# Experts two at a time, 32 places each, with each weight block read as one 8 KB row per partition

## The chip, the cores and the metric

The kernel runs on one core of one Trainium2 chip. The metric is device time in microseconds (us). TensorE does the matrix products (the profile calls it PE, and its weight loads PEld), VectorE is DVE, ScalarE is ACT, GpSimd is POOL, and SyncE is SP. SP issues nearly all transfers from HBM; 16 DMA engines carry them out.

## The reference

The program is three transformer blocks over 256 tokens of 1024 features, all in float32. The first two have a mixer of several attention kinds and a dense feed-forward part. The third has two attentions and then a mixture of 32 experts, which is the part that the change touches:

```
g_top = argmax(h @ w_group)                    # one of 4 groups per token
e_w, e_idx = top_k(softmax(h @ w_router of that group), 2)   # 2 of its 8 experts
for e in range(32):
    a = silu(h @ w_e_gate[e]) * (h @ w_e_up[e])   # 1024 -> 512
    out = out + gates[:, e] * (a @ w_e_down[e])   # 512 -> 1024
x = rmsnorm(x + out)
```

Every expert has three matrices of 2 MB, so that the experts' weights are 192 blocks of 1 MB (1024 KB each). A token uses only 2 of 32 experts, 16 tokens per expert on average; in the reference's routing of these inputs (seed 0) the fullest expert gets 24.

## The kernel before

The dense products of all blocks and the experts draw their weights from one stream (class `Stream`). A unit of it is up to 1 MB, kept in a place of 8 KB on each of the 128 partitions. `pump` issues transfers on SP's queue in the order of use, as long as there is a place; `free` gives a unit's place back after its last product, and calls `pump`. In the experts' stage there are 15 places, and three more (`LENT`) that serve for a single unit each. So a transfer can wait on SP for the product that last read its place.

`plan2` lists the experts' units: for each expert gate and up for the first 512 input features, gate and up for the other 512, then two units of the down matrix. The down units of the last two experts come last. A gate or up unit holds four rows of 2 KB on a partition, 128 matrix rows apart; a down unit two rows of 4 KB.

`route` finds for each token and expert the token's place among the expert's tokens. An expert has `CAP` = 64 places. `t_batch` gathers four experts at once: one-hot matrices on VectorE, and 32 products that lay the tokens' features on the partitions (`xe`, 256 columns, 64 for each expert); it also makes the matrices `gt` that bring results back. It runs as a side task, spread over the steps of the main loop. Nothing of the main loop starts before the first two pieces of batch 0.

`moe` (L2249) is the main loop, one expert at a time. For each of two halves of the input features, and each of four pieces of 128, it issues two products with 64 columns of stationary tokens and 512 moving columns of weights: gate into rows 0:64 of a PSUM bank, up into rows 64:128. These are two column tiles of TensorE. After the first half comes `emit_down` of the expert before (L2206), after the second `t_act` (tanh, two products on VectorE, four transposes, a copy on ScalarE), and after each second expert `emit_scatter` (L2233), four full-width products that add the results to the sum in PSUM. Before the last expert a branch on all engines (L2265) goes to `overflow` (L2043) if any expert has more than `CAP` tokens; that path runs every expert over all tokens again. `last_norm` (L2308) ends the program.

A float32 product of 512 columns shows as two records of the profile. Instructions issued through the class `Timed` all bear line 252, so that they are told apart by their tiles.

Of the kernel before, what the change touches and what calls it, by code (L numbers as in the profile page):

```python
# [13 lines left out]
P = 128  # L14
# [10 lines left out]
CAP = 64  # L25
NE = 32

# [21 lines left out]
LENT = 3  # units of the experts' weights that come into the arena while it has room  # L49
# [3 lines left out]
class Tables:  # L53
    """Tables that depend on the shapes alone, side by side: name -> (column, width)."""
# [17 lines left out]
def _tables():  # L72
    f = np.float32
    p, j = np.arange(P), np.arange(P)
    # for the whole program
# [7 lines left out]
    # for the first blocks  # L83
# [51 lines left out]
    # for the attention of the last block: distance to each key, or BIG where there is no such key  # L135
# [15 lines left out]
class Stream:  # L151
    """Weights in the order of their use: raw tiles come ahead by DMA, and the tiles of the dense
    products are split into two float32r parts a few pieces ahead of the product."""
# [24 lines left out]
    def pump(self, n=99):  # L178
        while self.issued < len(self.units) and self.slots and n:
            n -= 1  # L180
            self.held[self.issued] = self.slots.pop(0)
            view = self.slot(self.issued)
            for c, w, src in self.units[self.issued][2]:
                self.nc.sync.dma_start(out=view[:, :, c : c + w], in_=src)
            self.issued += 1
# [41 lines left out]
class Timed:  # L227
    """An engine whose instructions also move a rough clock, by which the order of emission is chosen."""
# [27 lines left out]
    def price(self, method, args, kw):  # L256
# [8 lines left out]
        if self.name == "PE":  # L265
            if method == "transpose":
                return 0.107 * n / 128
            if kw["lhsT"].dtype == F32R:
                return n / 2370 if n >= 256 else n / 600
            return max(0.213, n / 592) * (0.5 if out.shape[0] <= 64 else 1)  # L270
# [26 lines left out]
class Side:  # L297
    """Work that is emitted between the steps of the dense products: a step of a task when the steps
    before it are through by the rough clock, so that no engine's queue waits for another task."""

    def __init__(self):
# [6 lines left out]
        self.task = None  # [earliest start, end]; None: the dense products  # L308
        self.ahead = False  # weights are split ahead of their use
# [56 lines left out]
    def blocks(self, c0, dims, size):  # L366
        """The blocks of 8 bytes of a partition that an access touches."""
# [68 lines left out]
    def step(self, now):  # L436
        """Each task whose time has come goes on by a step."""
# [57 lines left out]
class Arena:  # L495
    """First-fit space in SBUF tiles; what may follow what is tracked by region."""
# [67 lines left out]
class Kernel:  # L564
# [26 lines left out]
    def split(self, hi, lo, ps, scale=1.0):  # L591
        """hi + lo = ps * scale, each a float32r."""
# [9 lines left out]
    def pow(self, out, in_):  # L602
        """in_ ** -0.5"""
# [24 lines left out]
    # groups of columns of the first blocks' w_in: (mode, name, column, width)  # L628
# [42 lines left out]

    def norm_row(self, k, gain):
        """Features k of x transposed, times their gain, in two parts."""
# [20 lines left out]
    def norm_rstd(self, rstd, ssq=None, scale=None):  # L694
        """(mean of the squares, times scale squared, + EPS) ** -0.5"""
# [49 lines left out]
    def banks(self, gi):  # L745
        """Four banks until the first norm is there, if there is room for it, then three of them."""
# [3 lines left out]
    def accs(self, segs, gi):  # L750
        """Accumulators of a group in two of the four banks of the dense products."""
# [53 lines left out]
    def t_wide(self):  # L805
        """rstd of each token along the free dimension, on all partitions."""
# [175 lines left out]
    def gelu2(self, out, x, tmp):  # L982
        """out = 2 gelu(x), tanh form; x may be in PSUM."""
# [12 lines left out]
    def rope(self, eng, z, n, which, dsts):  # L996
        """z [P, 2, n heads, 64] -> dsts (same shape)"""
# [21 lines left out]
    def t_qk(self, l):  # L1019
        """Rotated queries and keys, features on the partitions."""  # L1020
# [56 lines left out]
    def t_O(self, l):  # L1077
        """Room for the results of pairs of heads: two in a bank."""
# [12 lines left out]
    def t_branch(self, l, hp, br):  # L1091
        """Two heads of the selected or the window branch."""
# [68 lines left out]
        # back in their own place, the keys on the partitions  # L1161
# [18 lines left out]
    def t_pair(self, l, hp):  # L1180
        """The three branches' sum."""
# [11 lines left out]
    def t_gla(self, l):  # L1193
# [45 lines left out]
        # ex[:, i, 0]: level i (0: 128, 1..7: 64..1); ex[:, i, 1]: level i + 1, 7: 128  # L1239
# [182 lines left out]
    def t_params(self, l):  # L1422
        """Small parameters of a layer that need a transposition."""
# [36 lines left out]
    def next_norm(self, half, gain, l, tag):  # L1460
        """After half of x is final."""
# [21 lines left out]
    def norm_x(self, half):  # L1483
        """Half of x times the gains of the norm between the blocks, and its squares' sum."""
# [23 lines left out]
    def ffn(self, l, next_gain, next_tag):  # L1508
# [6 lines left out]
        for c in range(DFF // 256):  # L1515
            # gate and up, a bank each, the features on the partitions
# [9 lines left out]
            def go(c=c, g=g, u=u):  # L1526
                """silu(g) u in two parts"""
# [24 lines left out]
    def plan2(self):  # L1552
        """256 columns each: (mode, what, column)"""
# [14 lines left out]
        self.exp_units = [[] for _ in range(NE)]  # L1568

        def rows(e):  # L1570
            for h in range(2):
                for name in ("w_e_gate_2", "w_e_up_2"):
                    src = self.A[name][0][e][h * 512 : h * 512 + 512, :].rearrange("(k p) c -> p k c", p=P)
                    self.exp_units[e].append(self.st.add(512, 4, [(0, 512, src)], split=False))

        def down(e):
            for h in range(2):
                src = self.A["w_e_down_2"][0][e][h * 256 : h * 256 + 256, :].rearrange("(k p) c -> p k c", p=P)
                self.exp_units[e].append(self.st.add(D, 2, [(0, D, src)], split=False))

        for e in range(NE):
            rows(e)
            if e < NE - 2:
                down(e)
        down(NE - 2)
        down(NE - 1)
# [81 lines left out]
    def t_att(self, needs, groups, sink, slot, drops):  # L1668
        """Two heads: a softmax over the keys of all groups. groups: (queries, keys, values, distances,
        slopes of the two heads), each made when it is there."""  # L1670
# [79 lines left out]
        for gi, (need, q, k, v, dist, slopes) in enumerate(groups):  # L1750
# [6 lines left out]
            # back in their own place, the keys on the partitions  # L1757
# [79 lines left out]
    def mix2(self):  # L1837
        """x += (sigmoid(gate_d) (y_d W_d) + sigmoid(gate_s) (y_s W_s)) W_out"""
# [97 lines left out]
    def route(self):  # L1936
        """Of each token and expert: the place among the expert's tokens, from 1 (0: none), and the
        gate, which is made later."""
# [19 lines left out]
        def top(v, n, oh):  # L1958
            """The first of the largest of n: its value and its place as a one-hot."""
# [41 lines left out]
        # the group's share 1 / gs, of it the larger 1 / (1 + v), the other v / (1 + v)  # L2001
# [22 lines left out]
    def t_most(self):  # L2024
        """The largest place, in a register of each engine."""
# [581 lines left out]
```

## Time and profile before

| | |
|---|---|
| Time, median of 3 runs | 1522.21 us (1521.21 to 1523.0) |
| Span of the profiled execution | 1516.3 us, 5.9 below that median |
| TensorE busy | 1430.1 us, 94% of the span |
| VectorE, ScalarE, GpSimd busy | 52%, 39%, 15% |
| DMA | 360.78 MB, mean 238 GB/s |
| Experts' weights, by the size of their units | 192 x 1024 KB, 201.3 MB |

The span runs from the first to the last instruction. The page gives only the span of the profiled execution; the time of a run has launch and end around it, and the difference of 5.9 us is taken for that. Busy is the time in which an engine has any instruction under way. Matrix products overlap each other, so that a busy TensorE may still be able to do more. The DMA share is the time that packets took, summed over 16 engines; since packets overlap on an engine it can pass 1.

### The profile page before, as it was taken

How to read it: one execution, taken by the hardware profiler on the slowest of the kernel's cores; microseconds unless marked ns; L12 is line 12 of the kernel's file. 1: busy time of each engine (PE TensorE's matmuls, PEld its weight loads, DVE VectorE, ACT ScalarE, POOL GpSimd, SP SyncE). 2: the span in 40 equal slices, each digit the busy share in tenths (PEclk: the TensorE clock that was granted, in tenths of full speed). 3: DMA queues.
4: the chain of work that ended last, by engine and by line, in shares of the span. 5: the costliest groups of instructions: out<-in, count | busy, mean ns of one | idle time of the engine just before them, and what ended most of it. 6: DMA issues, size and time to landing. Idle time of an engine off the chain costs nothing. (4 is left out here: it accounts for less than half of the span.)

```text
span 1516.3 us, 23640 instructions
## 1 busy us (share of the span) xinstructions
PE 1430.1 (94%) x9055; PEld 1028.1 (68%) x9055; DVE 787.2 (52%) x1641; ACT 589.0 (39%) x1227; POOL 222.6 (15%) x341
## 2 busy tenths in 40 slices
PE   8789999999989999999999999979999999999996
PEld 7677999988767999988898998733333333333332
DVE  4487677756586777756766655642212121121212
ACT  5526655555535655555645465311111110111111
POOL 1144111101154111113523020110000000000000
PEclk9998999999999999999999999979999999999998
DMA  8652555547451556466344444879999999999993
GB/s 271 214 174 78 158 184 188 177 158 221 130 194 57 181 181 193 171 209 191 109 143 140 140 148 158 319 284 355 335 390 393 396 393 393 395 393 394 395 391 126
DMA packets 215049, 360.78 MB, mean 238 GB/s; under 512 B 8673, under 2 KB 106482, under 8 KB 214802
## 3 DMA queue, kind: packets, MB, share of 16 engines
q1 hardware_dynamic: 213362, 354.92, 66.9%
q0 software_dynamic: 1104, 3.58, 0.8%
q8 instruction: 72, 1.18, 0.3%
q10 hardware_dynamic: 464, 0.71, 0.1%
q14 instruction: 47, 0.39, 0.1%
HBM read 358.14 MB, written 1.05 MB: 237 GB/s over the span
## 5 line engine op out<-in xcount | busy, mean ns | idle before, releaser
L252 DVE TENSOR_TENSOR wlo<-raw,whi 128x512 fp32r<-128x512 f32 (+3 forms) x560 | 406.7, 734 | 263.1 <-ACT whi L252 251.0
L252 ACT CAST whi<-raw 128x512 fp32r<-128x512 f32 (+3 forms) x560 | 336.9, 605 | 351.2 <-PE psum L252 318.2
L252 PE MATMUL psum<-h_hi,whi 128*128 128x256 f32 x1040 | 296.1, 285 | 2.7 <-ACT whi L252 2.7
L252 PE MATMUL psum<-h_lo,whi 128*128 128x256 f32 x1040 | 290.8, 280 | 0.1
L252 PE MATMUL psum<-h_hi,wlo 128*128 128x256 f32 x1040 | 290.8, 280 | 0.0
L252 PE MATMUL psum<-raw,arena 128*64 128x512 f32 x712 | 227.0, 609 | 10.2 <-ACT arena L252 7.0
L252 DVE COPY arena<-psum 128x512 f32<-128x512 f32 (+4 forms) x96 | 57.4, 598 | 333.1 <-ACT arena L252 223.5
L252 PEld LDWEIGHTS psum<-h_hi,whi 128*128 128x128 f32 x1040 | 196.1, 189 | 10.0 <-issue 4.8
L252 PEld LDWEIGHTS psum<-h_lo,whi 128*128 128x128 f32 x1040 | 196.2, 189 | 0.9 <-issue 0.5
L252 PEld LDWEIGHTS psum<-h_hi,wlo 128*128 128x128 f32 x1040 | 196.0, 188 | 0.2 <-DVE wlo L252 0.2
L252 PE MATMUL psum<-raw_right,arena 128*64 128x512 f32 x504 | 166.3, 603 | 5.7 <-ACT arena L252 5.4
L252 ACT COPY arena<-psum 128x512 f32<-128x512 f32 (+3 forms) x89 | 48.2, 542 | 288.0 <-PE psum L252 275.0
L252 PE MATMUL psum<-arena 64*128 64x128 f32 (+11 forms) x732 | 144.8, 400 | 13.4 <-DVE arena L252 10.9
L252 PE MATMUL psum<-whi,h_hi 128*128 128x256 f32 (+3 forms) x448 | 146.0, 326 | 1.4 <-ACT arena_o L252 1.1
L252 PE MATMUL psum<-wlo,h_hi 128*128 128x256 f32 (+3 forms) x448 | 138.1, 308 | 0.0
L252 PE MATMUL psum<-whi,h_lo 128*128 128x256 f32 (+3 forms) x448 | 137.9, 308 | 0.0
L252 PEld LDWEIGHTS psum<-raw,arena 128*64 128x64 f32 x712 | 64.3, 139 | 97.1 <-issue 80.6
L252 PEld LDWEIGHTS psum<-arena 64*128 64x128 f32 (+4 forms) x732 | 75.2, 180 | 68.5 <-issue 42.4
L252 PE MATMUL psum<-raw_left,arena 128*64 128x512 f32 x296 | 111.4, 609 | 3.1 <-ACT arena L252 3.1
L252 ACT ACTIVATE arena<-psum 64x512 f32<-64x512 f32 (+3 forms) x70 | 33.7, 481 | 181.7 <-PE psum L252 175.8
L252 PEld LDWEIGHTS psum<-raw_right,arena 128*64 128x64 f32 x504 | 46.8, 137 | 72.6 <-issue 64.1
L252 PEld LDWEIGHTS psum<-whi,h_hi 128*128 128x128 f32 x448 | 85.1, 190 | 11.2 <-issue 4.3
(233 smaller groups left out, 1897.5 us busy)
## 6 DMA issues: line engine op xcount, KB each, us to landing
raw<-in_w_in_dram SPq DMA_DIRECT2D x76, 512.0 KB, 4.9
raw<-in_w_e_gate_dram SPq DMA_DIRECT2D x31, 1024.0 KB, 11.8
raw<-in_w_e_up_dram SPq DMA_DIRECT2D x31, 1024.0 KB, 10.0
raw<-in_w_e_down_dram SPq DMA_DIRECT2D x27, 1024.0 KB, 13.9
raw_right<-in_w_e_down_dram SPq DMA_DIRECT2D x23, 1024.0 KB, 13.0
raw<-in_w_gate_dram SPq DMA_DIRECT2D x44, 512.0 KB, 4.0
raw<-in_w_up_dram SPq DMA_DIRECT2D x44, 512.0 KB, 5.0
raw<-in_w_down_dram SPq DMA_DIRECT2D x20, 1024.0 KB, 5.1
```

Source lines behind the costliest of these rows:

```text
L252: return f(*args, **kw)
```

## The change

`CAP` becomes 32. Experts go in pairs (`q` of 16, `NQ = NE // 2`): four products at a time, gate and up of two experts, each with 32 stationary columns into its own 32 rows of the PSUM bank. A batch of the gather has eight experts of 32 places, a scatter serves four experts. The units come in the order gate, up of one expert, gate, up of the other, for each half; then four down units. Each unit is read as one run of 8 KB per partition (four neighbouring matrix rows instead of four that lie 128 apart), and the operands that meet it are taken with a step of 4, or 2, to match. The branch to `overflow` moves from before the last expert to the middle of the last pair, and `overflow` works with two places instead of four. The other edits remove comments and set the price that the order of emission uses for such a product.

```
-CAP = 64
+CAP = 32
+NQ = NE // 2
...
+                out = view[:, :, c : c + w]
+                if len(src.shape) == 2:
+                    out = self.held[self.issued][:, 0 : src.shape[1]]
+                self.nc.sync.dma_start(out=out, in_=src)
...
+            tiles = 4 if n == 512 and out.shape[0] <= 32 else 2 if out.shape[0] <= 64 else 1
+            return max(0.213, n / 592) / tiles
...
+        def rows(q):
             for h in range(2):
+                for e in (2 * q, 2 * q + 1):
+                    for name in ("w_e_gate_2", "w_e_up_2"):
+                        src = self.A[name][0][e][h * 512 : h * 512 + 512, :].rearrange("(p k) c -> p (k c)", p=P)
+                        self.exp_units[q].append(self.st.add(512, 4, [(0, 512, src)], split=False))
+        def down(q):
             for h in range(2):
+                for e in (2 * q, 2 * q + 1):
+                    src = self.A["w_e_down_2"][0][e][h * 256 : h * 256 + 256, :].rearrange("(p k) c -> p (k c)", p=P)
+                    self.exp_units[q].append(self.st.add(D, 2, [(0, D, src)], split=False))
...
-                    c = slice(tb * D + k * P, tb * D + k * P + P)
+                    c0 = tb * D + (k // 4) * 512
+                    c = slice(c0 + k % 4, c0 + 512, 4)
...
-            self.tr(ps[:, k * CAP : k * CAP + CAP], th[0:64, k * P : k * P + P])
+            c0 = (k // 2) * 256
+            self.tr(ps[:, k * 64 : k * 64 + 64], th[0:64, c0 + k % 2 : c0 + 256 : 2])
...
         for k in range(4):
             for c in range(2):
+                for x in range(2):
+                    w = self.st.slot(units[8 + k // 2 * 2 + x])[:, k % 2, :]
+                    o = r[c] + x * CAP
+                    self.mm(y[o : o + CAP, :], at[:, k, x * CAP : x * CAP + CAP], w[:, c * 512 : c * 512 + 512], k == 0, k == 3)
...
+        for q in range(NQ):
...
+                    for m in range(2):
+                        for x in range(2):
+                            o, c = m * 64 + x * CAP, (q % 4) * 64 + x * CAP
+                            self.mm(gu[o : o + CAP, :], xe[:, kk, c : c + CAP], self.st.slot(own[2 * x + m])[:, k, :], kk == 0, kk == 7)
...
+                for u in own:
+                    self.st.free(u)
+                if h == 0 and 1 <= q < NQ - 1:
+                    self.emit_down(q - 1)
+                if h == 0 and q == NQ - 1:
+                    S.until(("most",), ("gu", q - 1))
+                    with self.tc.If(self.most > CAP):
+                        self.overflow()
```

## Rows read from the trace of the kernel before

**Rows 1.** The page: busy tenths in 40 slices of 37.9 us.

```profile
PE   8789999999989999999999999979999999999996
DMA  8652555547451556466344444879999999999993
```

**Rows 2.** Busy time by stretches (us from the span's start), the experts' stage.

```profile
core 0: us, PE busy (x) PEld busy (x) DVE busy (x) ACT busy (x) POOL busy (x), PEclk, DMA share, GB/s
990.00:1000.00 10.00, 1.06 (x4) 0.93 (x4) 8.27 (x26) 3.44 (x5) 4.80 (x3) 0.50 1.05 397
1000.00:1010.00 10.00, 9.89 (x44) 6.15 (x45) 0.99 (x2) 1.17 (x2) 0.00 (x0) 0.72 0.30 120
1010.00:1110.00 100.00, 93.59 (x440) 36.49 (x438) 28.55 (x76) 13.11 (x25) 0.00 (x0) 0.98 0.94 346
1110.00:1470.00 360.00, 338.19 (x1524) 126.71 (x1520) 74.95 (x156) 44.66 (x85) 0.63 (x1) 1.00 1.04 394
```

**Rows 3.** TensorE in order of time, one expert: start, us, operation.

```profile
1294.33 7.09 PE L252 MATMUL psum<-raw,arena 128*64 128x512 f32 x32 [0.47 <-ACT arena L252]
1301.35 3.70 PE L252 MATMUL psum<-arena 128*128 128x512 f32 x8
1304.98 3.65 PE L252 MATMUL psum<-raw_right,arena 128*64 128x512 f32 x16
1308.56 0.46 PE L252 MATMUL psum<-tab,arena 64*128 64x64 f32 x4
```

**Rows 4.** TensorE in order of time, eight of a batch's 32 gathering products.

```profile
1272.14 0.39 PE L252 MATMUL psum<-onehot,h_hi 128*128 128x256 f32 x1
...
1273.06 0.28 PE L252 MATMUL psum<-onehot,h_lo 128*128 128x256 f32 x1
```

**Rows 5.** DMA packets: 1200 to 1206, 1209 to 1213, then 16.9 to 18.2 us.

```profile
DMA packets 1171, 2.31 MB, mean 386 GB/s; under 512 B 41, under 2 KB 41, under 8 KB 1171
...
DMA packets 442, 1.63 MB, mean 409 GB/s; under 512 B 19, under 2 KB 19, under 8 KB 442
...
DMA packets 105, 0.54 MB, mean 413 GB/s; under 512 B 12, under 2 KB 50, under 8 KB 50
```

**Rows 6.** TensorE and its weight loads near 100 us: products of `t_cmp`, 32 columns.

```profile
99.77 1.07 PE L252 MATMUL psum<-raw,arena_o 128*32 128x256 f32 x16
...
99.77 0.59 PEld L252 LDWEIGHTS psum<-raw,arena_o 128*32 128x32 f32 x16 [0.17 <-POOL arena_o L252]
...
L252 PE MATMUL psum<-raw,arena_o x128: 379/379/404, 99.8 to 444.9; 128*32 128x256 f32 x128
```

**Rows 7.** Transfers issued by SP, in order of time.

```profile
1009.60 0.37 SPq L252 DMA_DIRECT2D raw<-in_w_e_gate_dram  x1
...
1473.72 0.42 SPq L252 DMA_DIRECT2D raw_left<-in_w_e_down_dram  x1
```

**Rows 8.** TensorE in order of time, the stage's first products with experts' weights.

```profile
1003.79 2.79 PE L252 MATMUL psum<-raw,arena 128*64 128x512 f32 x8
...
1007.64 1.94 PE L252 MATMUL psum<-raw,arena 128*64 128x512 f32 x8
```

**Rows 9.** Busy time by stretches, the last transfers (columns as in rows 2).

```profile
1486.00:1488.00 2.00, 2.00 (x10) 0.66 (x8) 0.00 (x0) 0.00 (x0) 0.00 (x0) 0.79 0.70 287
1488.00:1490.00 2.00, 2.00 (x12) 0.68 (x10) 0.00 (x0) 0.00 (x0) 0.00 (x0) 1.00 0.23 94
```

**Rows 10.** The chain of work that ended last: start, us, what.

```profile
1480.92 17.65 PE psum L252 x60
...
1500.00 3.67 PE psum L252 x16
1503.67 0.02 issue
1503.69 0.59 ACT arena L252
1504.28 0.04 issue
1504.33 3.71 PE psum L252 x8
...
1511.36 0.72 ACT arena L252
```

More of the change, by code (lines that the diff above doesn't have):

```diff
@@ L1567, in plan2 @@
             self.plan_dense(None, [(0, 512, c * 512, self.A["w_out_2"][0])], 8, "out2")
-        self.exp_units = [[] for _ in range(NE)]
-        def rows(e):
+        self.exp_units = [[] for _ in range(NQ)]
+        def rows(q):
             for h in range(2):
[L1572 to L1576, printed above, removed]
-            for h in range(2):
[L1578 to L1586, printed above, removed]
+                for e in (2 * q, 2 * q + 1):
[3 more added lines that the diff above has]
+        def down(q):
+            for h in range(2):
+                for e in (2 * q, 2 * q + 1):
+                    src = self.A["w_e_down_2"][0][e][h * 256 : h * 256 + 256, :].rearrange("(p k) c -> p (k c)", p=P)
+                    self.exp_units[q].append(self.st.add(D, 2, [(0, D, src)], split=False))
+        for q in range(NQ):
+            rows(q)
+            if q < NQ - 2:
+                down(q)
+        down(NQ - 2)
+        down(NQ - 1)
     def t_final_norm(self):
@@ L2048, in overflow @@
         ov = new((2, NE))
-        w = [t.rearrange("p (k c) -> p k c", k=4) for t in self.st.slots[:4]]
-        assert self.st.issued == len(self.st.units) and len(w) == 4
+        w = [t.rearrange("p (k c) -> p k c", k=4) for t in self.st.slots[:2]]
+        assert self.st.issued == len(self.st.units) and len(w) == 2
         xg = new((NK, T))
@@ L2083, in overflow @@
             for k in range(4):
-                ps = self.ps(5 + k % 2)[:, 0:256]
+                ps = two[k % 2][:, 0:256]
                 for tb in range(2):
@@ L2091, in overflow @@
                 for tb in range(2):
-                    ps = self.ps(5 + tb)
+                    ps = two[tb]
                     for k in range(4):
@@ L2119, in t_batch @@
         d = self.onehot[:, b % 2]
[L2120 removed]
+        e0 = b * 8
         for tb in range(2):
             nc.vector.tensor_tensor(
[L2123 to L2125 removed]
+                out=d[:, tb].rearrange("p (e s) -> p e s", e=8),
+                in0=self.place[:, tb, e0 : e0 + 8].unsqueeze(2).to_broadcast([P, 8, CAP]),
+                in1=self.tab("iota").unsqueeze(1).to_broadcast([P, 8, CAP]),
                 op=ALU.is_equal,
             )
[L2128 removed]
+        xe = self.xe[b] = yield from self.ar.new(NK, 8 * CAP)
         hi = self.h_hi.rearrange("p a b -> p (a b)")
@@ L2151, in t_batch @@
             self.gates()
-        dg = yield from self.ar.new(2, 2, 3, CAP)
+        dg = yield from self.ar.new(2, 2, 3, 2 * CAP)
         for tb in range(2):
             for pr in range(2):
-                for i in range(3):
-                    e = e0 + 2 * pr + i % 2
+                for i in range(6):
+                    e = e0 + 4 * pr + i % 4
                     nc.vector.tensor_scalar(
-                        out=dg[:, tb, pr, i, :],
+                        out=dg[:, tb, pr, i // 2, i % 2 * CAP : i % 2 * CAP + CAP],
                         in0=self.tab("iota"),
@@ L2180, in t_batch, with t_act @@
         self.gt[b] = gt
-    def t_act(self, e, bank):
+    def t_act(self, q, bank):
         nc, S = self.nc, self.side
@@ L2192, in t_act @@
         nc.vector.tensor_tensor(out=th[0:64], in0=th[0:64], in1=gu[64:128], op=ALU.mult)
-        S.done.add(("gu", e))
+        S.done.add(("gu", q))
         yield
@@ L2203, in t_act, with emit_down @@
         self.ar.drop(th)
-        self.at[e] = at
-    def emit_down(self, e):
+        self.at[q] = at
+    def emit_down(self, q):
         nc, S = self.nc, self.side
-        S.until(("act", e))
-        units = self.exp_units[e]
-        at = self.at.pop(e)
+        S.until(("act", q))
+        units = self.exp_units[q]
+        at = self.at.pop(q)
         y = self.ps(6)
-        odd = e % 2
+        odd = q % 2
         if not odd:
             self.Y = self.ar.now(2, 512)
-        r = [slice(64, 128) if c ^ odd else slice(0, 64) for c in range(2)]
+        r = [64 * (c ^ odd) for c in range(2)]
         for k in range(4):
-            w = self.st.slot(units[4 + k // 2])[:, k % 2, :]
             for c in range(2):
-                self.mm(y[r[c], :], at[:, k, :], w[:, c * 512 : c * 512 + 512], k == 0, k == 3)
+                for x in range(2):
+                    w = self.st.slot(units[8 + k // 2 * 2 + x])[:, k % 2, :]
+                    o = r[c] + x * CAP
+                    self.mm(
+                        y[o : o + CAP, :], at[:, k, x * CAP : x * CAP + CAP], w[:, c * 512 : c * 512 + 512], k == 0, k == 3
+                    )
             if k % 2:
-                self.st.free(units[4 + k // 2])
-        nc.scalar.copy(out=self.Y[r[0], 0], in_=y[r[0]])
-        nc.vector.tensor_copy(out=self.Y[r[1], 1], in_=y[r[1]])
+                for x in range(2):
+                    self.st.free(units[8 + k // 2 * 2 + x])
+        nc.scalar.copy(out=self.Y[r[0] : r[0] + 64, 0], in_=y[r[0] : r[0] + 64])
+        nc.vector.tensor_copy(out=self.Y[r[1] : r[1] + 64, 1], in_=y[r[1] : r[1] + 64])
         self.ar.drop(at)
@@ L2231, in emit_x, with emit_scatter @@
                 self.mm(self.ps(c * 2 + tb), self.ident, self.x[:, tb, c * 512 : c * 512 + 512], False, False)
-    def emit_scatter(self, pair):
-        self.side.until(("batch", pair // 2))
-        gt = self.gt[pair // 2]
+    def emit_scatter(self, quad):
+        self.side.until(("batch", quad // 2))
+        gt = self.gt[quad // 2]
         for c in range(2):
@@ L2239, in emit_scatter @@
                     self.ps(c * 2 + tb),
-                    gt[:, pair % 2, c, tb * P : tb * P + P],
+                    gt[:, quad % 2, c, tb * P : tb * P + P],
                     self.Y[:, c],
-                    pair == 0,
-                    pair == NE // 2 - 1,
+                    quad == 0,
+                    quad == NQ // 2 - 1,
                 )
         self.ar.drop(self.Y)
-        if pair % 2:
-            self.ar.drop(self.gt.pop(pair // 2))
+        if quad % 2:
+            self.ar.drop(self.gt.pop(quad // 2))
     def moe(self):
@@ L2252, in moe @@
         self.xe, self.gt, self.at = {}, {}, {}
-        nb = NE // 4
+        nb = NQ // 4
         S.start(self.t_batch(0), ("batch", 0))
         self.ar.drop(self.xg)
-        for e in range(NE):
-            b = e // 4
+        for q in range(NQ):
+            b = q // 4
             S.until(("xe", b, 3 if b else 1))
-            if e == 4:
+            if q == 2:
                 S.start(self.t_most(), ("most",))
-            if e % 4 == (1 if b else 2) and b + 1 < nb:
+            if q % 4 == (1 if b else 2) and b + 1 < nb:
                 S.start(self.t_batch(b + 1), ("batch", b + 1))
-            if e == NE - 1:
-                S.until(("most",))
-                with self.tc.If(self.most > CAP):
-                    self.overflow()
             xe = self.xe[b]
-            bank = 4 + e % 2
+            bank = 4 + q % 2
             gu = self.ps(bank)
-            if e >= 2:
-                S.until(("gu", e - 2))
-            units = self.exp_units[e]
+            if q >= 2:
+                S.until(("gu", q - 2))
+            units = self.exp_units[q]
             for h in range(2):
-                wg, wu = self.st.slot(units[2 * h]), self.st.slot(units[2 * h + 1])
+                own = units[4 * h : 4 * h + 4]
                 S.until(("xe", b, 2 * h + 1))
@@ L2289, in moe @@
+            if q % 4 == 3:
                 self.ar.drop(self.xe.pop(b))
-            act = self.t_act(e, bank)
-            if e == NE - 1:
+            act = self.t_act(q, bank)
+            if q == NQ - 1:
                 next(act)
                 next(act)
-                self.emit_scatter(e // 2 - 1)
-                self.emit_down(e - 1)
-            S.start(act, ("act", e), -1)
-            if 2 <= e < NE - 2 and e % 2 == 0:
-                self.emit_scatter(e // 2 - 1)
+                self.emit_scatter(q // 2 - 1)
+                self.emit_down(q - 1)
@@ L2299, in moe @@
+            S.start(act, ("act", q), -1)
+            if 2 <= q < NQ - 2 and q % 2 == 0:
+                self.emit_scatter(q // 2 - 1)
                 S.tick()
-            if e == NE // 2:
+            if q == NQ // 2:
                 self.emit_x()
-            if e == NE - 4:
+            if q == NQ - 2:
                 self.gfin = self.ar.now(D)
                 nc.gpsimd.dma_start(out=self.gfin, in_=self.A["g_final_2"].unsqueeze(0).to_broadcast([P, D]))
-        self.emit_down(NE - 1)
+        self.emit_down(NQ - 1)
```

41 lines of the change are left out of this document (15 added, 26 removed).

## Prediction

> **What bounds the kernel now.** I read the slices of the page first: from slice 28 on both TensorE and the DMA engines are at nine tenths [rows 1]. That is the experts' stage, the only one that the change touches, and two engines look full in it. The busy times by stretches say which one is [rows 2]. From 1110 to 1470 us the 16 DMA engines have a share of 1.04 and move 394 GB/s without a dip. An expert is six units of 1.0486 MB, 6.29 MB, so the transfers take 16.0 us for it.
>
> TensorE's need for the same expert comes from its records in order of time [rows 3, 4]. The 32 records of gate and up run in pairs: 7.09 us, less the 0.59 that one record lasts, over 15 steps is 0.43 us a pair. Down is 16 records more: 24 pairs, 10.3 us. Transposes and the wait ahead of the next product make 1.0 (0.46, and 0.47 idle). A scatter of 3.70 serves two experts: 1.85. A batch has four times the eight products that run from 1272.14 to 1273.34, 4.8 us, and some 2.5 of transposes and waits, for four experts: 1.8. Sum 15.0 us of 16.0. So TensorE is nearly full too, and one engine relieved alone would gain little: with the transfers faster TensorE would bind 6% on, with TensorE faster nothing would move in the long stretch.
>
> Around this stretch are two losses. From 1010 to 1110 the transfers make 346 GB/s instead of 394 [rows 2], 100 x (1 - 346/394) = 12.2 us lost: TensorE begins with every place full, and gives them back one expert at a time, so SP waits for places. And at the end the last packets land at about 1489.5 [rows 9] and the span ends at 1516.3: 26.8 us, in which TensorE works off its backlog [rows 10].
>
> **What 8 KB rows do.** The packets show it: where the rows are 2 KB the core gets 386 GB/s, in a stretch that is nearly all 4 KB rows 409, and early in the kernel, where a table with rows of 9000 B (55 of 105 packets, 92% of the bytes) comes in, 413 [rows 5]. An engine then spends 16 x 2048 B / 386 = 84.9 ns on a 2 KB packet and 160.2 on 4 KB: 75.3 for each 2 KB and 9.6 for the packet. Estimate for 8 KB from these two: 4 x 75.3 + 9.6 = 310.8 ns, 422 GB/s. Lower end: no better than 4 KB rows, 409. The nearest row, 9000 B, lies at 413 with small packets among them; I take 417. That packets of that length go out whole is in the same row.
>
> The Trainium skill, "DMA: Bandwidth & Descriptors", section "Why small descriptors are slow", gives a fixed overhead of about 3 cycles per packet beside one cycle for each 32 B. By that rule 2 KB rows would cost 67 cycles for 64 of data and 8 KB rows 259 for 256, so the mixture of today would gain 2.7%. The rows 386 and 409 lie 6% apart where the rule has 2.3%, so the trace does not bear the rule out in size; it stands below as a rival.
>
> **What four column tiles do.** The group of four products has eight records. That four tiles run at once is in this trace: `t_cmp` has 32-column products on four column tiles, and 16 records of 256 columns take 1.07 us although one lasts 0.379 [rows 6]: (1.07 - 0.38) / 3 = 0.23 us from one four to the next, about half of the 0.43 that a pair of 512 columns takes. Their 16 weight loads fit into 0.59 us. So four records of 512 columns step at 0.43, and a pair of experts needs 24 x 0.43 = 10.3 for its products, as one expert did. With transposes 1.0, scatter 3.70/2 and batch 7.3/4 that is 15.0 us of TensorE for a pair against 12 x 1.0486/0.417 = 30.2 us of transfers. Upper end for this: pairs overlap but fours don't, 25.3 us, still below 30.2. TensorE is out of the way in the stage at either end.
>
> Less work on VectorE and ScalarE (half as many `t_act`) gains nothing: they are busy 21% and 12% of the stretch [rows 2]. The same holds for eight scatters less. The 96 small operations that make `dg` remain as many, hidden by transfers. The strided operands of the gather and of the transposes are unknown in price: from nothing to a doubling. In the stage the idle half of TensorE covers it; ahead of the first expert 16 gathering products stand on the path, at 0.15 us each [rows 4], twice that at half clock: 0 to 5 us. I take 0, since the number of elements loaded is the same.
>
> **Do the places suffice?** Places now come back four at a time. When the fourth unit of a half lands, eight of 15 places hold data (these four, and the four down units before them); seven are on SP's queue, 17.6 us of transfers. TensorE needs 3.4 us for the half (6.9 at half clock) to free four, then down frees four more. The queue doesn't run dry.
>
> **The sum.** The first places come back at 1009.60 today, when the first half of expert 0 is done [rows 7, 8]. The first half of a pair is as many steps, so this stays. By then 18 units are in. The other 174, 182.5 MB, take 437.5 us at 417 GB/s. With 2 us to get going (the queue was empty) and 2 at the end, where the 16 engines run out unevenly [rows 9], the last packet lands at 1009.6 + 2 + 437.5 + 2 = 1451. The same sum for today: 1009.6 + 2 + 182.5/0.394 (463.2) + 12.2 + 2 = 1489.0, against 1489.5 seen.
>
> Behind the last packet: the last 8 units, 20 us of transfers, are down matrices, and TensorE does everything up to the last half of them while they come: second half, scatter, down of pair 14, some 12 us. The branch stands between the halves of the last pair, where TensorE waits 10 us for units anyway; without that cover it would cost the few us it costs today. What is left: about 1 us until the landing is seen, four steps of the last down (1.7, at half clock 3.4; take 2.5), the copy 0.6 with its gaps, then as today from 1504.33, the scatter, the norm and the output, 12.0 us [rows 10]. The scatter's 3.7 may run partly at half clock: 1.8 more. Sum 18, bounds 15 to 22. Span 1451 + 18 = 1469, plus 5.9 for what lies around it: **1475 us**. The gain of 47 is 25.7 from the rate, 12.2 from the head and 8.8 from the end.
>
> **The rivals.**
> (a) *Rows of 8 KB do no better than 4 KB rows.* 182.5/0.409 = 446.1: 8.6 later, 1484. For it: 409 and 413 lie close. Against: the fixed part of a packet is plain between 2 and 4 KB.
> (b) *The gain in rate is half or none.* Rate of today: 463.2 instead of 437.5, 1501. That the rows come as short packets after all would show the same; against it is the 9000 B row. The skill's rule named above would be a case between: 463.2/1.027 = 451.0, 1488.5.
> (c) *TensorE falls to half clock through the stage.* With 15 us of work in 30 it idles in each pair, up to 12 us while down units come, and an idle TensorE does drop: in 990 to 1000, with 1.06 us busy, the granted clock was 0.50, and 0.72 in the ten us after [rows 2]. If it never rose again, a pair would need 30.0 us: no more than the transfers, but the margin would be gone, and the end at half clock is 7 longer; with 5 of stalls 1487. Against: the bursts of each pair are dense, and in rows 2 it was back at 0.98 within the next stretch. The Trainium skill, "TensorE: Matmul & The Clock Gate", section "HAM oscillation", describes this as a loop whose bursts between waits for DMA each start at 1.2 GHz. The row of 990 to 1000 agrees that idling leads to 1.2 GHz.
> (d) *The four tiles run one after another: slower.* Then a pair's 96 records take 96 x 0.43 = 41.3, with 4.7 around them 46 us, against two of today's 16.0. 16 x (46 - 32) = 224 more: about 1740. It decides from 24 steps of (32 - 4.7)/24 = 1.14 us instead of 0.43. Against it: rows 6.
> (e) *An expert has more than 32 tokens*, and `overflow` runs: over 200 MB of weights again, 500 us or more. The fullest has 24 by the reference, so it is a remainder.
> (f) *Nothing moves*, since a wait that I don't see replaces what is gained.
>
> **How the numbers follow.** Forecast 0.60, for 1466 to 1483 (rate 422 to 410, tail 15 to 22). Rival (a) 0.15, (b) 0.12, (c) 0.07, (d) 0.03, (e) 0.01, (f) 0.02. The range must leave out no more than 0.2: 1464 to 1492 holds the forecast, (a), (c), and the page's rule of (b), and leaves out no gain in rate and (d) to (f). A difference under 0.2%, 3 us, is about what a measurement of this kernel can't tell from none. Faster: forecast, (a), (b), (c), 0.94. Same: (f), 0.02. Slower: (d), (e), 0.04.
>
> **What would show it.** DMA packets of 8 KB, and 410 to 422 GB/s from 1010 us to the end without a dip; TensorE busy near half instead of 94%, with waits for DMA in place of SP's waits for TensorE; groups of four records stepping at 0.43 us; the last packet near 1451 and 18 us of work behind it. Wrong it would be if the rate stays under 400, if the DMA share dips below 1 in the stage (places), if the records of a group of four don't overlap, or if the clock is near 0.5 and TensorE still above 90% busy.

## The result, and the profile after

The changed kernel takes 1482.34 us (median of 4 runs, 1480.5 to 1483.66) against 1521.71 for the kernel before on the same chip (4 runs, 1515.17 to 1523.0). The ratio is 0.9749, with a 95% interval from 0.9726 to 0.9772. The forecast was 1475 in a range of 1464 to 1492, so the time lies 7 us above the forecast and inside the range. The profiled execution took 1483.14 us with a span of 1481.4.

The page of the changed kernel, against [rows 1]: busy tenths, granted TensorE clock, DMA share and GB/s in 40 slices (now of 37.0 us), and the sizes of the packets.

```profile
PE   7789999999989999999999999978776757766576
...
PEclk9899999999999999999999999998888868787778
DMA  8743466555533465567434353697999999899995
GB/s 262 233 129 101 153 189 182 177 197 173 173 120 110 154 189 185 172 198 224 144 115 143 117 170 114 205 372 308 419 421 420 369 421 420 351 420 420 420 416 235
DMA packets 157703, 360.73 MB, mean 244 GB/s; under 512 B 8673, under 2 KB 106482, under 8 KB 132882
```

24,821 packets (157703 less 132882) are now 8 KB or longer; before there were 247. In the experts' stage, slices 28 to 37 counted from 0, the rate is 419 to 421 GB/s and TensorE is down from nine tenths to five to seven. But two of these slices read 369 and 351. The busy times by stretches put numbers on this; the columns are those of [rows 2].

```profile
1000.00:1010.00 10.00, 7.32 (x37) 5.56 (x38) 3.30 (x15) 0.89 (x3) 0.00 (x0) 0.61 0.52 218
1010.00:1110.00 100.00, 80.35 (x489) 30.53 (x491) 23.00 (x76) 8.57 (x16) 0.00 (x0) 0.88 0.96 398
1110.00:1200.00 90.00, 60.77 (x318) 22.06 (x315) 13.78 (x38) 6.04 (x11) 0.00 (x0) 0.77 0.97 400
1200.00:1300.00 100.00, 70.75 (x398) 26.29 (x394) 13.79 (x38) 6.81 (x13) 0.00 (x0) 0.80 0.96 394
1300.00:1400.00 100.00, 63.04 (x356) 17.26 (x348) 8.23 (x12) 5.84 (x11) 0.63 (x1) 0.81 1.01 420
```

The undisturbed stretch, 1300 to 1400, has 420 GB/s. At that rate 1110 to 1200 lost 90 x (1 - 400/420) = 4.3 us and 1200 to 1300 lost 6.2: two gaps, 10.5 us together. Both show as a DMA rate of zero. Here is the rate around each in 40 slices, first from 1140 to 1180 us (1 us each), then from 1270 to 1300 (0.75 us each).

```profile
GB/s 410 442 410 426 410 442 418 401 434 401 442 418 401 434 410 442 418 197 74 16 0 82 246 418 401 451 426 426 418 426 442 418 401 442 410 451 393 418 434 410
...
GB/s 448 415 426 393 426 437 415 426 404 426 426 426 448 382 415 328 87 87 0 0 0 0 0 153 175 360 415 437 415 448 404 459 404 448 404 382 459 404 448 393
```

Why the first one happens stands in two queues. SP's issues in order of time, as in [rows 7], show nothing issued for 20 us:

```profile
1140.17 0.38 SPq L256 DMA_DIRECT2D raw_right<-in_w_e_gate_dram  x1
1160.71 0.33 SPq L256 DMA_DIRECT2D raw_right<-in_w_e_up_dram  x1
```

TensorE in order of time over those 20 us, as in [rows 3, 4], and then VectorE between 1147 and 1155:

```profile
1142.06 0.40 PE L256 MATMUL psum<-onehot,h_lo 128*128 128x256 f32 x1
1142.29 0.40 PE L256 MATMUL psum<-onehot,h_hi 128*128 128x256 f32 x1
...
1146.37 0.44 PE L256 MATMUL psum<-onehot,h_lo 128*128 128x256 f32 x1
1148.49 0.47 PE L256 MATMUL psum<-tab,arena 128*128 128x128 f32 x1 [1.68 <-DVE arena L256]
1150.96 0.90 PE L256 MATMUL psum<-tab,arena 128*128 128x128 f32 x3 [2.00 <-DVE arena L256]
1152.54 1.11 PE L256 MATMUL psum<-tab,arena 128*128 128x128 f32 x4 [0.68 <-ACT arena L256]
1155.82 0.74 PE L256 MATMUL psum<-tab,arena 64*128 64x64 f32 x4 [2.16 <-DVE arena L256]
1157.03 3.64 PE L256 MATMUL psum<-raw_right,arena 128*32 128x512 f32 x16 [0.47 <-ACT arena L256]
```
```profile
1147.52 5.04 DVE L256 TENSOR_SCALAR arena<-tab,place,g 128x32 f32<-128x32 f32 x24
```

What counts here is the order. After the first half of a pair, the next thing that frees places is the down product of the pair before (1157.03). It needs that pair's four transposes of hidden activations (1155.82). In front of these stands a block of the next batch's gather: 24 gathering products, 24 operations on VectorE that make `dg` (5.04 us), and eight transposes (128x128). SP had issued seven units ahead, 17.6 us of transfers, and the block lasts longer, so the queue runs dry at about 1157. The same block, and the same pause of SP, follow at 1266 to 1287, for the next batch.

The clock adds to each gap. When TensorE comes to the down products, its granted clock is 0.50, the lower of its two levels (busy times by stretches, columns as in [rows 2]; the third line is the same kind of work outside the gaps):

```profile
1157.00:1160.00 3.00, 2.97 (x16) 0.78 (x20) 0.00 (x0) 0.00 (x0) 0.00 (x0) 0.50 0.25 96
1283.00:1286.00 3.00, 2.96 (x16) 0.78 (x20) 0.00 (x0) 0.00 (x0) 0.00 (x0) 0.50 0.03 14
1297.00:1298.70 1.70, 1.70 (x16) 0.52 (x20) 0.00 (x0) 0.00 (x0) 0.00 (x0) 1.00 1.05 439
```

So 16 records take 3.64 us at 1157.03, and 1.92 at 1296.97. By this estimate some 1.7 us of each gap are the clock's; no run tests it alone.

Three more readings. Gathering products start 0.23 us apart (1142.06 to 1142.29, at a granted clock of 1.00), where before it was 0.117 (six steps from the line below to 1273.06 in [rows 4], also at 1.00): the price of the step that I had set at nothing.

```profile
1272.36 0.28 PE L252 MATMUL psum<-onehot,h_lo 128*128 128x256 f32 x1
```

Places return at 1013.69 instead of 1009.60 [rows 7]. And the end, by the chain of work that ended last, against [rows 10]:

```profile
1465.22 3.60 PE psum L256 x14
...
1468.85 0.59 ACT arena L256
...
1469.48 3.71 PE psum L256 x8
...
1476.52 0.72 ACT arena L256
```

The last packets land at about 1464.5 (stretches, columns as in [rows 2]), so 16.9 us stand behind them:

```profile
1464.00:1464.50 0.50, 0.00 (x0) 0.00 (x0) 0.00 (x0) 0.00 (x0) 0.00 (x0) 1.00 0.12 49
1464.50:1465.00 0.50, 0.00 (x0) 0.00 (x0) 0.00 (x0) 0.00 (x0) 0.00 (x0) 1.00 0.00 0
```

### The profile page after: what moved, and what is told of

Read it like the earlier page. It is cut to its first block, busy times and chain, and to the rows that moved or that the text cites. A ratio compares the mean times of both kernels' runs of the same rounds, so it can differ in the third digit from the quotient of the medians.

```text
span 1481.4 us, 22857 instructions
## 1 busy us (share of the span) xinstructions
PE 1290.3 (87%) x8767; PEld 964.5 (65%) x8767; DVE 740.4 (50%) x1573; ACT 558.6 (38%) x1167; POOL 223.5 (15%) x341
## 2 busy tenths in 40 slices
DMA packets 157703, 360.73 MB, mean 244 GB/s; under 512 B 8673, under 2 KB 106482, under 8 KB 132882
## 5 line engine op out<-in xcount | busy, mean ns | idle before, releaser
L256 PE MATMUL psum<-raw,arena 128*32 128x512 f32 x704 | 177.2, 683 | 60.6 <-DMA raw<-in_w_e_gate_dram 49.5
L256 DVE COPY arena<-psum 128x384 f32<-128x384 f32 (+4 forms) x68 | 38.0, 559 | 351.1 <-ACT arena L256 239.6
L256 PE MATMUL psum<-raw_right,arena 128*32 128x512 f32 x496 | 144.0, 670 | 23.6 <-DMA raw_right<-in_w_e_gate_dram 16.9
L256 PEld LDWEIGHTS psum<-raw,arena 128*32 128x32 f32 x704 | 38.2, 120 | 148.0 <-DMA raw<-in_w_e_gate_dram 64.5
L256 PE MATMUL psum<-raw_left,arena 128*32 128x512 f32 x312 | 107.0, 684 | 28.0 <-DMA raw_left<-in_w_e_gate_dram 22.2
L256 PE MATMUL psum<-arena 64*128 64x256 f32 (+10 forms) x668 | 116.0, 381 | 13.5 <-DVE arena L256 11.5
L256 ACT COPY arena<-psum 128x384 f32<-128x384 f32 (+3 forms) x61 | 32.0, 525 | 225.3 <-PE psum L256 220.8
L256 ACT ACTIVATE arena<-psum 128x256 f32<-128x256 f32 (+3 forms) x38 | 18.1, 477 | 237.0 <-PE psum L256 236.9
L256 PEld LDWEIGHTS psum<-arena 64*128 64x128 f32 (+4 forms) x668 | 64.1, 180 | 48.9 <-issue 22.0
L256 POOL TENSOR_TENSOR arena<-arena 128x512 f32<-128x512 f32 (+2 forms) x46 | 49.2, 1079 | 298.5 <-DVE arena L256 286.5
```

Of the source, the lines that this page charges most:

```text
L256: return f(*args, **kw)
```

## The experiments

All ratios are to the kernel before on the same chip: 1521.49 us (11 runs, 1515.9 to 1528.8) for the first four, 1519.33 (17 runs, 1515.43 to 1526.83) for the last four. My theory at this point: the rate and the pairing bring the gain, as predicted, and what is missing are the two gaps, made by the order on TensorE's queue. The rivals: the gaps come from TensorE's half clock, or the transfers pause by themselves; and the gain comes from the rows or the pairs alone.

**e1: rows of 8 KB in the kernel before, without the pairs.**

```
-  src = ...[h * 512 : h * 512 + 512, :].rearrange("(k p) c -> p k c", p=P)
+  src = ...[h * 512 : h * 512 + 512, :].rearrange("(p k) c -> p (k c)", p=P)
-  c = slice(tb * D + k * P, tb * D + k * P + P)
+  c = slice(c0 + k % 4, c0 + 512, 4)        # stationary operand with a step
```

> The kernel before with one part of the change: weight blocks read as one 8 KB row per partition, with the strided operands; experts stay single, 64 places, two column tiles. My theory is that either engine alone was nearly the bound, 15.0 us of TensorE against 16.0 us of transfers for an expert: the transfers would then make 420 GB/s where there is a place, but TensorE binds, at 15.0 to 15.4 us an expert, 10 to 18 us in all: 1503 to 1511 us. Rival, the rate is all of the gain: about 26 us, 1495. If the rows do not matter: 1521.

Measured: 1566.05 us (1563.59 to 1567.91), ratio 1.0285 (1.0248 to 1.0322). It is 45 us slower than before, a miss for every theory. Its stretches of the stage and its gathering weight loads (1110 to 1440 us; operation, shape, count, busy us, mean ns):

```profile
1010.00:1110.00 100.00, 94.37 (x381) 42.91 (x377) 21.84 (x58) 11.21 (x22) 0.00 (x0) 0.93 0.74 290
1110.00:1470.00 360.00, 339.39 (x1380) 142.51 (x1379) 73.42 (x162) 41.02 (x78) 0.00 (x0) 0.95 0.90 359
```
```profile
L255 PEld LDWEIGHTS psum<-onehot,h_lo 128*128 128x128 f32 x68 | 22.4, 330 | 0.0
L255 PEld LDWEIGHTS psum<-onehot,h_hi 128*128 128x128 f32 x67 | 21.7, 324 | 13.8 <-issue 8.2 <-DVE arena L255 3.2 <-ACT arena L255 2.4
```

An expert takes 6.29 MB/359 = 17.5 us with TensorE 94% busy, so TensorE sets the pace. A new theory follows: a stationary operand with a step of four elements nearly doubles its weight load, from 0.19 to some 0.33 us, and the product waits for it. An expert has eight gathering products, each 0.117 later, and a group of transposes, with a step of two, 0.23 longer (0.69 against 0.46 in [rows 3]): 1.17 us, 37 for 32 experts. e5 tests this.

**e2: the pairs with rows as before.**

```
-  ...rearrange("(p k) c -> p (k c)", p=P)          # gate, up, down
+  ...rearrange("(k p) c -> p k c", p=P)
-  c = slice(c0 + k % 4, c0 + 512, 4)
+  c = slice(tb * D + k * P, tb * D + k * P + P)     # and no step in the transposes
```

> The changed kernel with the weight blocks read as before (rows of 2 and 4 KB, 128 or so rows apart, operands without a step); pairs, 32 places and four column tiles stay. By my theory the transfers bind at 394 GB/s: 182.5 MB take 463 us instead of 434, the two gaps in the transfers shrink as the queue lasts longer, and the time is 1501 to 1509 us, 13 to 20 under the kernel before. Rival, the gain is TensorE's: about 1482, as the whole change.

Measured: 1497.6 us (1496.71 to 1499.27), ratio 0.9843 (0.9808 to 0.9878).

```profile
1030.00:1110.00 80.00, 55.87 (x316) 17.16 (x318) 11.39 (x35) 5.24 (x10) 0.00 (x0) 0.77 1.04 392
1300.00:1400.00 100.00, 60.40 (x308) 15.26 (x304) 6.17 (x9) 4.66 (x9) 0.63 (x1) 0.76 1.04 394
```

With TensorE relieved the transfers keep 394 GB/s, the rate of [rows 2], and now hold it from the head of the stage. So the rows of 2 and 4 KB cap the rate at 394, and the rows of 8 KB are what lifts it to 420 (e7, below, takes no step either and has 420). Whether this comes from the length of the rows or from the order of their addresses, no run separates. The two gaps shrink as expected, to some 2.4 us together (389 GB/s from 1110 to 1300). The time is 3 us below the range that was expected; the profiled execution came to the router's last products, the end of the dense part, at 995.73, 6.1 us before the changed kernel's.

**e3: the batch's gather started behind the down products.**

```
-            if q % 4 == (1 if b else 2) and b + 1 < nb:
-                S.start(self.t_batch(b + 1), ("batch", b + 1))
...          # after self.emit_down(q - 1):
+                    if q % 4 == (1 if b else 2) and b + 1 < nb:
+                        S.start(self.t_batch(b + 1), ("batch", b + 1))
```

> The changed kernel with one line moved: the gather of the next batch is started after the down products of the pair before, not at the top of the pair. Theory: the two gaps of 5 us in the transfers come from the order on TensorE's queue (24 gathering products, 24 operations of VectorE and 8 transposes stand ahead of the transposes and the down products that give places back), so they go: 9 to 11 us less, 1471 to 1474. Rival 1, the half clock makes the batch long wherever it stands: the gaps stay at half their size or more, 1477 to 1482. Rival 2, the transfers pause by themselves (memory, instruction loading): no change, 1482.

**e4: the activation of a pair started before the places of its second half are freed**, which puts its transposes ahead of the batch's block.

```
+                if h == 1 and q < NQ - 1:
+                    S.start(self.t_act(q, bank), ("act", q), -1)
                 for u in own:
                     self.st.free(u)
...
-            S.start(act, ("act", q), -1)       # for the pairs before the last
```

> The changed kernel with another line moved: the activation of a pair is queued before the second half's places are given back, so that the planner takes its start from the last product and not from a transfer's landing; the batch starts where it did. The same theory: the activation's transposes then stand ahead of the gather, the places come back in time, the two gaps go, 1471 to 1474. Rival 1: gaps stay at half or more, since the gather still stands in the middle of the first half, 1477 to 1482. Rival 2: no change, 1482.

Measured: e3 1468.25 us (1463.38 to 1471.59), ratio 0.9647 (0.9618 to 0.9676); e4 1469.46 (1465.45 to 1473.23), ratio 0.9653 (0.9623 to 0.9682). The stretches of e3, then of e4:

```profile
1110.00:1200.00 90.00, 64.75 (x356) 23.32 (x355) 13.87 (x38) 6.28 (x12) 0.00 (x0) 0.81 1.01 420
1200.00:1300.00 100.00, 65.34 (x324) 23.12 (x324) 13.18 (x37) 5.85 (x11) 0.00 (x0) 0.78 1.01 420
```
```profile
1110.00:1200.00 90.00, 67.00 (x378) 23.62 (x370) 15.16 (x40) 7.00 (x13) 0.00 (x0) 0.83 1.01 420
1200.00:1300.00 100.00, 73.27 (x390) 25.66 (x382) 15.24 (x40) 7.39 (x14) 0.00 (x0) 0.85 1.01 420
```

Two different edits of the order, the same work, and both gaps are gone: 420 GB/s in each stretch. The clock is 0.78 to 0.85, about that of the changed kernel (0.77 and 0.80), so a lowered clock alone makes no gaps, and the transfers don't pause by themselves. Both times lie below the expected 1471 to 1474, by 2.8 and 1.5. In the profiled executions the router's last products come at 995.82 and 998.92 against 1001.81 in the changed kernel's, 6.0 and 2.9 earlier, in work that neither edit touches. With the 10.5 of the gaps that makes 16.5 and 13.4 of the 17.2 and 13.4 by which the spans are shorter. Both kernels are faster than the changed one.

**e5, e6, e7: contiguous stationary operands.** The features are permuted once, where the normed tokens (`xgr`) and the hidden activations (`th`) are written, so that the gather and the transposes take no step. e5 is e1 with this edit, e6 is e3 with it, e7 is the changed kernel with it, its order of TensorE's work otherwise kept.

```
-            out=self.xgr[:, :, s],
-            in0=self.x[:, :, s],
+            out=self.xgr[:, :, s].rearrange("p t (j q) -> p t j q", j=4),
+            in0=self.x[:, :, s].rearrange("p t (q j) -> p t j q", j=4),
...
-                    c = slice(c0 + k % 4, c0 + 512, 4)
+                    c = slice(tb * D + k * P, tb * D + k * P + P)
...
+        tv = th[0:64].rearrange("p (c j q) -> p c j q", c=2, j=2)   # tanh and products write tv
-            self.tr(ps[...], th[0:64, c0 + k % 2 : c0 + 256 : 2])
+            self.tr(ps[...], th[0:64, k * P : k * P + P])
```

> The kernel before with rows of 8 KB per partition, as in e1_rows_only, but every stationary operand stands contiguous: the permutation of rows is made where the gathered tokens and the hidden activations are written, so TensorE loads no operand with a step of four elements. Theory (the step doubles the weight loads and made TensorE the bound at 17.5 us per expert in e1): gather product back from 0.41-0.43 to about 0.28-0.31 us, TensorE near 15.0-15.4 us per expert, transfers at about 420 GB/s where they are fed; 1503 to 1512 us. Rival (rows of 8 KB harm the order of the work or the places by themselves, the step is innocent): stays near 1560. Rival (the rate is all that matters once the step is gone): about 1495.

Measured: 1520.55 us (1516.79 to 1523.45), ratio 1.0007 (0.9988 to 1.0026). The gathering loads are back at 188 ns, and the 45 us that e1 lost are back too, all but one; of these 37 were worked out above, and the rest stays open. That the step is what e1 paid for is shown. But 1503 to 1512 was expected, and the time is that of the kernel before. Its loads, its stage, and its waits from 1110 to 1470 us (us in total, times, longest), first TensorE's and then SP's:

```profile
L255 PEld LDWEIGHTS psum<-onehot,h_lo 128*128 128x128 f32 x80 | 15.1, 188 | 0.0
```
```profile
1110.00:1470.00 360.00, 337.89 (x1506) 126.33 (x1504) 75.72 (x178) 44.07 (x84) 0.63 (x1) 0.99 0.98 399
```
```profile
PE psum L255 <- ACT arena L255: 14.2, 27, 0.7
PE psum L255 <- DVE arena L255: 7.9, 10, 2.2
...
SPq L255 <- PE psum L255: 303.3, 100, 11.1
```

TensorE waits for no transfer at all in 360 us; its 22 us of waits are for ScalarE and VectorE. SP waits 303 us for places that TensorE holds. So TensorE binds, and an expert takes it 6.29 MB/399 = 15.8 us, its waits included, where I had 15.0. The kernel before has nearly the same waits in the same stretch, first TensorE's and then SP's:

```profile
PE psum L252 <- ACT arena L252: 14.2, 27, 0.7
PE psum L252 <- DVE arena L252: 7.6, 10, 2.2
...
SPq L252 <- PE psum L252: 221.4, 93, 6.6
```

There too TensorE waits for no transfer, here or anywhere else from its first product with experts' weights to the end, and from that product to the end both kernels take the same time: 512.5 us (1003.79 to 1516.3) and 512.7 (1005.97 to 1518.7). So TensorE set the pace of the kernel before as well, at 6.29 MB/394 = 16.0 us an expert, and the transfers' limit for its rows, 394 by e2, lay at that very rate.

> e3_batch_later (pairs, 8 KB rows, the batch's gather behind the pair's down products) with contiguous stationary operands. Theory (the doubled loads are hidden behind the transfers once the gather no longer stands before the act): the same as e3_batch_later, 1465 to 1468 us, 419 to 420 GB/s throughout. Rival (the gather products are still on the path that sets the end): 1458 to 1463 us.

Measured: 1468.65 us (1465.58 to 1471.16), ratio 0.9661 (0.9628 to 0.9693), the same as e3. Where the transfers bind and the gather stands behind the down products, the doubled loads cost nothing that can be measured.

> The change itself, its order of TensorE's work left as it is, with contiguous stationary operands. Theory (the two gaps are the time by which the gather group before the act outlasts the transfers already queued): 24 gather products at 0.117 to 0.234 us apart and the transposes shorten the group by some 3 to 4 us, the gaps of about 5 us each shrink to 1 to 3 us; 1474 to 1478 us. Rival (the group is paced by VectorE's 24 operations of about 0.2 us, not by the loads): gaps stay, 1480 to 1483 us.

Measured: 1470.04 us (1467.99 to 1475.59), ratio 0.9677 (0.965 to 0.9704), 12 below the changed kernel (11 by the ratios) and some 4 better than the theory said. The rate around the two gaps, same slices as for the changed kernel:

```profile
GB/s 418 426 418 434 401 434 410 418 434 418 418 410 418 352 213 172 426 426 352 393 360 418 418 410 434 434 434 401 442 434 426 401 434 426 385 426 418 418 434 418
...
GB/s 415 437 415 404 437 404 371 218 76 11 153 208 448 382 448 382 426 437 437 437 426 404 404 437 404 426 437 404 459 371 426 437 415 459 371 415 437 426 448 393
```

Against 420 GB/s, the slices below 400 among the 14th to the 21st lose 1.6 us in the first gap, the 7th to the 12th lose 2.7 in the second. So 10.5 us of gaps became some 4.2, as expected: 6.3 gained. SP's pause before the first shrinks from 20.5 to 17.6 us (1136.19 to 1153.82). The other 6.4 between the two profiled executions lie outside: places return 3.5 us earlier (1010.14 instead of 1013.69), and the last down products happen to run at full clock, 1.95 us instead of 3.60. The rest, 1.2, stays open.

**e8: the kernel before, profiled again.**

> The kernel before, unchanged, profiled once more for the spread of its head: the first expert product between 1003 and 1010 us, the time 1 to 3 us above its own span, between 1515 and 1529 us. If the head moves by several us between executions of one program, the 4.1 us by which the dense part of the changed kernel came later are no effect of the change; if it stays within 1 us, they are.

Measured: 1523.67 us, span 1520.8. SP's first issue when places return:

```profile
1011.77 0.37 SPq L252 DMA_DIRECT2D raw<-in_w_e_gate_dram  x1
```

That is 2.2 us later than in [rows 7], and its first expert product comes at 1006.8, 3.0 later than in [rows 8], in one and the same program. The router's last products, the end of the dense part, come at 1001.26 against 998.18, 3.1 later. Over all profiled executions they come between 995.73 (e2) and 1002.29 (e1). The time was 2.9 us above the execution's own span, 1.7 in the changed kernel's.

## Why the prediction was nearly right

**What bounds the kernel: right that both are nearly full, wrong in which sets the pace.** "One engine relieved alone would gain little" held sharply: rows alone, without the step, gain nothing (e5), pairs alone 1.6% (e2), both with a better order 3.5% (e3). But the prediction let the transfers bind, with TensorE 1 us an expert below them, and faster transfers gain until "TensorE would bind 6% on". The traces show TensorE setting the pace of the kernel before already. Its term was mis-sized: 15.8 to 16.0 us per expert instead of 15.0, in e5 14.8 busy and 1.0 of waits for ScalarE and VectorE. The forecast survived this because the changed kernel's time was summed from its own transfers.

**8 KB rows: right.** 420 GB/s in undisturbed stretches, where I took 417 and had estimated 422 from the fixed part of a packet. A packet takes 16 x 8192 B/420 = 312 ns. Rival (a), 409, and rival (b) fall. From e2's rows to the changed kernel's the rate rises by 6.6%. The rule of the Trainium skill, "DMA: Bandwidth & Descriptors", section "Why small descriptors are slow", gives an estimate of 2.7% for this; the measurement does not agree in size.

**Four column tiles: right.** TensorE in order of time, a group of four records and the first of the next:

```profile
1028.21 0.59 PE L256 MATMUL psum<-raw_right,arena 128*32 128x512 f32 x1
1028.22 0.59 PE L256 MATMUL psum<-raw,arena 128*32 128x512 f32 x1
1028.23 0.59 PE L256 MATMUL psum<-raw_right,arena 128*32 128x512 f32 x1
1028.23 0.59 PE L256 MATMUL psum<-raw,arena 128*32 128x512 f32 x1
1028.64 0.59 PE L256 MATMUL psum<-raw_right,arena 128*32 128x512 f32 x1
```

Four records start within 0.02 us, and the next four 0.43 later. Rival (d) falls.

**The clock, rival (c): the fall came, most of its price did not.** The granted clock is 0.77 to 0.81 in the stretches from 1110 to 1400, between its two levels (0.50 and 1.00 of full speed), and TensorE now waits for units: 49.5 us for gate units in one of the three buffers alone, in 12 waits between 1010 and 1440. The Trainium skill, "TensorE: Matmul & The Clock Gate", section "HAM oscillation", describes such bursts between waits for DMA; the trace agrees. But e3 holds 420 GB/s from 1030 to 1400 at 0.78 to 0.87, so by itself it costs the transfers nothing. What it costs in the changed kernel is some 1.7 us of each gap, by the estimate above, and the last down products, 3.60 us where the prediction took 2.5.

**"I take 0" for the strided operands: the wrong end of the bounds.** The upper one, a doubling, was near: loads go from 188 to some 328 ns, the spacing of the products from 0.117 to 0.23. In the head, where the prediction looked for it, the price is small: 6.0 us instead of 5.6 from the router's last products to the first expert product. "In the stage the idle half of TensorE covers it" failed: there it made 6.3 us of the gaps (e7).

**"The queue doesn't run dry": this step failed.** Seven units queued, 17.6 us, was right. What TensorE does until the next place returns was not 3.4 to 6.9 us. At the second and the third batch the block of the gather came first, 20 us from 1140.17 to 1160.71. I had put the batch down as 7.3 us spread over four steps, and hadn't asked where in the emitted order it would come to stand. e3 and e4 show that without this order there are no gaps, with the same work; e7 shows that with this order the longer loads made 6.3 of their 10.5 us.

**The sum.** Against the predicted span of 1469: places returned 4.1 later, the gaps cost 10.5, 182.5 MB at 420 instead of 417 give back 3.0, getting going and running out take the 1.8 that is left between places' return and the last packet (5.8 for 4), and the tail is 1.1 shorter (16.9 for 18). That is 12.3, against 12.4 measured. Of the head's 4.1, 3.6 arose before the router's last products (1001.81 against 998.18), in work that the change doesn't touch; e8 shows a shift of nearly that size, 3.1, without any change. In the other direction, my 5.9 us "around the span" mixed two executions: the profiled span of before, 1516.3, was a short one, and within one execution the difference is 1.7 (changed kernel) to 2.9 (e8). That is 4.2 less for the profiled one. 1475 + 12.3 - 4.2 = 1483.1, its time. So the error, 8 us in this execution and 7 in the median, is 10.5 of gaps that I hadn't foreseen, less 2.3 for rate and end; that head and surroundings nearly cancel is luck.

## What to carry to other kernels

When a tile's places come back in larger groups, list everything that can stand on the engine's queue between two groups, side tasks included, and compare it with the transfers already queued; a planner that ranks by due times can put a whole side task there. Before costing two nearly full engines, look which of them waits for the other, count the waits into each one's pace as well as its busy time, and expect a gain only where both are relieved. Make a permutation where an operand is written, not where TensorE loads it as stationary, unless transfers cover the load.

## What was unexpected of the hardware

A float32 stationary operand of 128x128 read with a step of four elements loads in 324 to 332 ns instead of 187 to 189, and the products behind it then start 0.23 us apart instead of 0.117. A 64x128 operand with a step of two took 209 ns instead of 141 (e1, e5). Where TensorE binds the steps cost 43 us (e1 and e5, each against the kernel before on its chip). Writing the permuted order on VectorE, GpSimd and ScalarE instead left no cost that could be measured (e6 against e3). And one and the same dense part ended at times up to 6 us apart: the router's last products come at 995.82 in e3 and 1001.81 in the changed kernel.
